# Grouped keys and queries of block 1's attention, loaded in pieces of 32 rows in place of 64

## The chip, the cores and the metric

The kernel runs on one core of one Trainium2 chip. Its time is the device time of one execution in microseconds (us); the times below are of three runs, with their median. The profile is of one further execution of the same kernel.

## What is computed

Three transformer blocks run one after the other on one sequence of 512 tokens with 1024 channels, all in float32. The change lies in the first. Its middle part projects the normalized input and runs two kinds of attention on it side by side, eight heads each:

```python
proj = h @ w_in[l]
qa, ka, va, qb, kb, vb = [proj[..., offs[i]:offs[i + 1]] for i in range(6)]
...
oa = diff_attention(qa[:, :, 0], qa[:, :, 1], ka[:, :, 0], ka[:, :, 1], va, lam, rel_bias)
...
qb = rms_norm(qb.reshape(B, S, N_HEADS_B, HEAD_DIM), q_norm[l]).transpose(0, 2, 1, 3)
kb = rms_norm(kb.reshape(B, S, N_KV_B, HEAD_DIM), k_norm[l]).transpose(0, 2, 1, 3)
qb = apply_rope(qb, cos, sin)
kb = apply_rope(kb, cos, sin)
ob = gqa_attention(qb, kb, vb).transpose(0, 2, 1, 3).reshape(B, S, D_MIX_B)
x = x + jnp.concatenate([oa, ob], axis=-1) @ w_out[l]
```

`gqa_attention` is the grouped one: eight query heads of 64 channels share two key heads, four to one. These grouped keys and queries are what the change loads in another way.

## The kernel before

Activations lie with channels on the 128 partitions and the 512 tokens along the row. Every float32 product is made of rounded parts: `weight` (L124) loads a weight panel into one of three `wraw` buffers, ScalarE rounds it to `whi` (L137), VectorE takes the rest as `wlo` (L138), and TensorE multiplies the parts in three matmuls (L120 to L122) that accumulate in a PSUM bank, named a to h.

Block 1's attention is `mix1` with `heads1` (from L563), some 240 us of the execution from about 420 us on. A head's operands go through DRAM, since matmul operands must lie on other partitions than the projection leaves them on. `parts` (L488) takes a projected and rotated chunk of 128 channels, writes its rounded value and its rest into a buffer `hl` (ScalarE L493, VectorE L494; there are two such buffers, `HL = 2`), and stores the buffer to DRAM (L499). The stored tensors are `qdd` and `kdd` for the first kind of attention, `qpd` and `kpd` for the grouped queries and keys; in each a row of DRAM is one channel, 512 values of the rounded part and then 512 of the rest. Operands are then loaded from there, one head ahead of their use:

- `keys` (L593) fills two `kg` tiles for a key head, one with the rounded parts, one with the rests, each with the head's 64 channels twice, on partitions 0 to 63 and 64 to 127.
- `ahead_gqa` (L678) fills a `qg` tile for a query head: rounded parts on partitions 0 to 63, rests on 64 to 127. On the first head of a group it calls `keys` before that.
- `operand` (L610) loads the `qd` and `kd` tiles of the first kind in pieces of 32 partitions (L614).

A head's 64 channels are 32 even ones and 32 odd ones, which lie 64 rows apart in DRAM. So one load of 64 partitions reads two runs of 32 rows; its access pattern `[(64, 2), (1, 32)]` says: 2 runs, 64 rows apart, of 32 rows, one apart. `part_rows` (L502) makes the pattern, with the 512 values of a row as the last dimension. Each load moves 64 rows of 2 KB, 128 KB. There are 8 loads of kg and 16 of qg.

The score matmuls are L627 (first kind, operands kd and qd) and L651 (grouped, operands kg and qg), both into banks a and b in turn. VectorE reduces the scores (L629, L652), ScalarE takes the exponential (L485). Beside the first heads run the value projections `v_tokens` (L505), into banks c to f, which ScalarE and VectorE empty into `vt` (L518, L519).

All of these loads and stores are issued by SyncE (SP), in one order. The order of the instructions on each engine is set by a scheduler when the kernel is built, and each engine then works through its own list. SP's DMAs take eight completion semaphores in turn, so that a DMA is issued only when the one eight places ahead of it has landed, beside what it waits for in its data and its buffer.

Of the kernel before, what the change touches and what calls it, by code (L numbers as in the profile page):

```python
# [29 lines left out]
def f32v(ap):  # L30
    return ap.bitcast(F32)


class K:
    NU = 5
    SECOND = ("dq", "pf", "ct", "cacc")
    out = "out"
# [525 lines left out]
    def heads1(self, xhl, rb, rtok, gq, ind, ocs):  # L563
        nc, D = self.nc, self.D
# [26 lines left out]
        d = []  # L591

        def keys(kv):  # L593
            ds = []
            for i in range(2):
                t = self.keep("kg", 3, F32R)
                for r in range(2):
                    nc.sync.dma_start(out=f32v(t[64 * r:64 * r + 64]), in_=self.part_rows(d[0], i, 32 * kv, [(64, 2), (1, 32)]))
                ds.append(t)
            return ds  # L600

# [55 lines left out]
        qds, kds, qgd = {}, {}, {}  # L657
# [20 lines left out]
        def ahead_gqa(c, r):  # L678
            if r == 0 and c % 2 == 0:
                kg[c // 2] = keys(c // 2)  # L680
            t = self.keep("qg", 2, F32R)
            for i in range(2):
                nc.sync.dma_start(out=f32v(t[64 * i:64 * i + 64]), in_=self.part_rows(qgd[c], i, 32 * r, [(64, 2), (1, 32)]))
            ops[4 + c, r] = t

        def mk_diff(c, r):
            if r == 1:
                qgd[c + self.AH] = rope(c + self.AH, "qpd") if c < 4 - self.AH else None
            ahead_gqa(c, r)
            return diff_head(2 * c + r, sms[c], *ops[c, r])  # L690
# [1434 lines left out]
```

## Time and profile before

| | us |
|---|---|
| median of three runs | 2681.27 |
| the three runs | 2675.64, 2681.27, 2682.28 |
| the profiled execution, its own time | 2672.23 |
| its span in the trace | 2670.5 |
| TensorE busy in it (PE) | 2596.1 |
| VectorE busy (DVE) | 1575.7 |
| ScalarE busy (ACT) | 1054.2 |
| GpSimd busy (POOL) | 403.6 |

Times in the trace are counted from the start of the span. PE stands for TensorE's matmuls, PEld for its weight loads, which overlap them; SPq is SyncE's queue, where the duration shown is that of issuing a DMA, not of its transfer. A row of the timeline has the start, the duration, the engine, the line of the kernel, the operation, its output and inputs, and, in square brackets, how long the engine was idle before it and whom it waited for. A row of the chain of waits has the start, the length and the piece of work that held up the end there. A row of a stretch has its length, the busy time and instruction count of each engine, then the granted TensorE clock as a share of full speed, the mean busy share of the core's 16 DMA engines, and the GB/s that they moved.

### The profile page before, as it was taken

How to read it: one execution, taken by the hardware profiler on the slowest of the kernel's cores; microseconds unless marked ns; L12 is line 12 of the kernel's file. 1: busy time of each engine (PE TensorE's matmuls, PEld its weight loads, DVE VectorE, ACT ScalarE, POOL GpSimd, SP SyncE). 2: the span in 40 equal slices, each digit the busy share in tenths (PEclk: the TensorE clock that was granted, in tenths of full speed). 3: DMA queues.
4: the chain of work that ended last, by engine and by line, in shares of the span. 5: the costliest groups of instructions: out<-in, count | busy, mean ns of one | idle time of the engine just before them, and what ended most of it. 6: DMA issues, size and time to landing. Idle time of an engine off the chain costs nothing.

```text
span 2670.5 us, 31163 instructions
## 1 busy us (share of the span) xinstructions
PE 2596.1 (97%) x11804; PEld 2097.3 (79%) x11804; DVE 1575.7 (59%) x2446; ACT 1054.2 (39%) x1621; POOL 403.6 (15%) x331
## 2 busy tenths in 40 slices
PE   8999998989999999999999999999899899999999
PEld 6887887767788887988788777888788777878787
DVE  7876655788644544467434854333545977746564
ACT  4222233676422324455323533223433464424242
POOL 1011012233000003133112201001210313101000
PEclk9999998989999999999999999999999999999999
DMA  5566644432632234431323342322524644323323
GB/s 196 178 200 202 205 155 148 138 104 96 209 95 95 88 102 134 137 111 65 97 99 128 134 144 93 97 96 96 187 69 149 209 103 158 95 91 94 99 88 111
DMA packets 114594, 340.00 MB, mean 127 GB/s; under 512 B 13784, under 2 KB 15768, under 8 KB 114314
## 3 DMA queue, kind: packets, MB, share of 16 engines
q1 hardware_dynamic: 104010, 301.02, 34.7%
q0 software_dynamic: 10432, 36.97, 4.4%
q8 instruction: 93, 1.52, 0.2%
q14 instruction: 59, 0.48, 0.1%
HBM read 301.47 MB, written 40.67 MB: 128 GB/s over the span
## 4 chain that ended last, share of the span: by engine, by line
PE 89%; DVE 5%; DMA 2%; ACT 2%; issue 1%; POOL 0%; SPq 0%; POOLq 0%; DVEq 0%; ACTq 0%
PE a L121 5%; PE a L120 5%; PE a L122 5%; PE e L122 4%; PE c L120 4%; PE c L122 4%; PE c L121 4%; PE e L120 4%; PE e L121 4%; PE f L120 4%; PE f L121 4%; PE f L122 4%; PE b L122 4%; PE b L120 4%; PE b L121 4%; PE d L120 4%
## 5 line engine op out<-in xcount | busy, mean ns | idle before, releaser
L137 ACT ACTIVATE whi<-wraw 128x1024 fp32r<-128x1024 f32 (+4 forms) x420 | 423.9, 1012 | 1048.5 <-PE e L121 172.2
L138 DVE TENSOR_TENSOR wlo<-wraw,whi 128x1024 fp32r<-128x1024 f32 (+5 forms) x408 | 494.7, 1214 | 326.0 <-ACT whi L137 320.1
L122 PE MATMUL e<-xh,wlo 128*128 128x512 f32 x368 | 144.1, 392 | 1.6 <-DVE wlo L138 1.6
L120 PE MATMUL e<-xh,whi 128*128 128x512 f32 x368 | 144.2, 392 | 0.0
L121 PE MATMUL e<-xl,whi 128*128 128x512 f32 x368 | 144.1, 392 | 0.0
L121 PE MATMUL a<-xl,whi 128*128 128x512 f32 x352 | 139.2, 396 | 2.3 <-DVE xl L194 2.0
L120 PE MATMUL a<-xh,whi 128*128 128x512 f32 x352 | 138.8, 394 | 0.2 <-ACT xh L911 0.2
L122 PE MATMUL a<-xh,wlo 128*128 128x512 f32 x352 | 138.1, 392 | 0.3 <-DVE wlo L138 0.3
L121 PE MATMUL c<-xl,whi 128*128 128x512 f32 x344 | 135.3, 393 | 2.5 <-DVE xl L194 2.5
L120 PE MATMUL c<-xh,whi 128*128 128x512 f32 x344 | 135.5, 394 | 0.9 <-ACT whi L137 0.9
L122 PE MATMUL c<-xh,wlo 128*128 128x512 f32 x344 | 135.0, 393 | 0.0
L120 PE MATMUL b<-xh,whi 128*128 128x512 f32 x304 | 119.7, 394 | 6.7 <-ACT xh L193 6.7
L121 PE MATMUL b<-xl,whi 128*128 128x512 f32 x304 | 119.7, 394 | 0.0
L122 PE MATMUL b<-xh,wlo 128*128 128x512 f32 x304 | 119.4, 393 | 0.0
L190 ACT ACTIVATE hh<-h 128x512 fp32r<-128x512 f32 x98 | 61.8, 630 | 144.0 <-DVE h L369 92.4
L122 PE MATMUL f<-xh,wlo 128*128 128x512 f32 x280 | 109.9, 392 | 0.6 <-DVE wlo L138 0.6
L942 POOL TENSOR_TENSOR acc<-sq 128x512 f32<-128x512 f32 x10 | 14.1, 1406 | 637.8 <-ACT sq L296 371.2
L120 PE MATMUL f<-xh,whi 128*128 128x512 f32 x280 | 110.2, 394 | 0.0
L121 PE MATMUL f<-xl,whi 128*128 128x512 f32 x280 | 109.3, 390 | 0.0
L122 PE MATMUL d<-xh,wlo 128*128 128x512 f32 x264 | 103.9, 394 | 2.0 <-DVE wlo L138 2.0
L120 PE MATMUL d<-xh,whi 128*128 128x512 f32 x264 | 104.3, 395 | 0.0
L121 PE MATMUL d<-xl,whi 128*128 128x512 f32 x264 | 103.7, 393 | 0.0
(1182 smaller groups left out, 6446.0 us busy)
## 6 DMA issues: line engine op xcount, KB each, us to landing
wraw<-w_up SPq DMA_DIRECT2D x76, 512.0 KB
mw<-w_mod POOLq DMA_DIRECT2D x48, 512.0 KB, 4.3
wraw<-ffn_w_gate SPq DMA_DIRECT2D x43, 512.0 KB
wraw<-ffn_w_up SPq DMA_DIRECT2D x43, 512.0 KB
wraw<-w_down SPq DMA_DIRECT2D x40, 512.0 KB
wraw<-ffn_w_down SPq DMA_DIRECT2D x32, 448.0 KB
wraw<-w_gate SPq DMA_DIRECT2D x24, 512.0 KB
wraw<-ffn_w_down SPq DMA_DIRECT2D x16, 512.0 KB
```

The costliest lines, as they stand in the source:

```text
L120: mm(out, ah, bh, start=(first and i == 0), stop=False)
L121: mm(out, ah, bl, start=False, stop=False)
L122: self.last_mm = mm(out, al, bh, start=False, stop=(last and i == n - 1)).ins
L137: nc.scalar.activation(hi[:, i:j], raw[:, i:j], AF.Copy)
L138: (nc.gpsimd if self.pool_lo else nc.vector).tensor_sub(lo[:, i:j], raw[:, i:j], f32v(hi[:, i:j]))
L190: nc.scalar.activation(hi, x, AF.Copy)
L942: i = (self.nc.vector if c == 6 else self.nc.gpsimd).tensor_add(a, acc, s).ins
```

## The change

Both loops issue two loads of 32 partitions for each that had 64, one for the even channels and one for the odd ones; what lands where is the same.

```diff
             for i in range(2):
                 t = self.keep("kg", 3, F32R)
                 for r in range(2):
-                    nc.sync.dma_start(out=f32v(t[64 * r:64 * r + 64]), in_=self.part_rows(d[0], i, 32 * kv, [(64, 2), (1, 32)]))
+                    for a in range(2):
+                        nc.sync.dma_start(out=f32v(t[64 * r + 32 * a:64 * r + 32 * a + 32]), in_=self.part_rows(d[0], i, 32 * kv + 64 * a, [(1, 32)]))
                 ds.append(t)
             return ds
...
             t = self.keep("qg", 2, F32R)
             for i in range(2):
-                nc.sync.dma_start(out=f32v(t[64 * i:64 * i + 64]), in_=self.part_rows(qgd[c], i, 32 * r, [(64, 2), (1, 32)]))
+                for a in range(2):
+                    nc.sync.dma_start(out=f32v(t[64 * i + 32 * a:64 * i + 32 * a + 32]), in_=self.part_rows(qgd[c], i, 32 * r + 64 * a, [(1, 32)]))
             ops[4 + c, r] = t
```

On TensorE, VectorE, ScalarE and GpSimd every instruction keeps its place (their lines below the edits count one or two higher). SP's list grows from 788 to 812 instructions. Its rows at the first grouped head, where kpd and qpd are stored and read back, were these before:

```order
L499 DMA kpd<-hl 128x1024
L598 DMA kg<-kpd 64x1x512 x4
L169 DMA wraw<-w_v 128x960
L598 DMA kg<-kpd 64x1x512 x2
L499 DMA qpd<-hl 128x1024
L499 DMA qdd<-hl 128x1024
L683 DMA qg<-qpd 64x1x512 x3
L169 DMA wraw<-w_v 128x640
L683 DMA qg<-qpd 64x1x512
L499 DMA kdd<-hl 128x1024
L169 DMA wraw<-w_in 128x1024
```

The same place in the changed kernel, with L598 now L599 and L683 now L685:

```order
L499 DMA kpd<-hl 128x1024
L599 DMA kg<-kpd 32x512 x8
L169 DMA wraw<-w_v 128x960
L599 DMA kg<-kpd 32x512 x4
L499 DMA qpd<-hl 128x1024
L499 DMA qdd<-hl 128x1024
L685 DMA qg<-qpd 32x512 x4
L169 DMA wraw<-w_v 128x640
L685 DMA qg<-qpd 32x512
L499 DMA kdd<-hl 128x1024
L685 DMA qg<-qpd 32x512 x3
L169 DMA wraw<-w_in 128x1024
```

Twelve pieces in place of six loads stand ahead of the store of qpd, and three of the second query head's four pieces have moved behind the store of kdd. Later, where the second key head is loaded, SP had these rows before:

```order
L620 DMA btab<-be_2029 128x896
L598 DMA kg<-kpd 64x1x512 x2
L683 DMA qg<-qpd 64x1x512 x2
L499 DMA qpd<-hl 128x1024
L614 DMA qd<-qdd 32x2x512 x3
```

And in the changed kernel:

```order
L621 DMA btab<-be_2029 128x896
L599 DMA kg<-kpd 32x512 x4
L685 DMA qg<-qpd 32x512 x4
L499 DMA qpd<-hl 128x1024
L615 DMA qd<-qdd 32x2x512 x3
```

Here eight pieces stand for four loads, and the order of the rest is as it was.

## The prediction

> **What bounds the kernel now.** I began with the page: its first line, the row of engines and the chain of what ended last.
>
> ```profile
> span 2670.5 us, 31163 instructions
> PE 2596.1 (97%) x11804; PEld 2097.3 (79%) x11804; DVE 1575.7 (59%) x2446; ACT 1054.2 (39%) x1621; POOL 403.6 (15%) x331
> ...
> PE 89%; DVE 5%; DMA 2%; ACT 2%; issue 1%; POOL 0%; SPq 0%; POOLq 0%; DVEq 0%; ACTq 0%
> ```
>
> TensorE sets the end; DMA holds 2% of the chain. A change that only touches loads can win no more than the places where TensorE stands still for one, directly or through another engine. So I read the chain in order of time over block 1's attention, about 420 to 660 us.
>
> ```profile
> 434.24 0.65 DVE hl L494 x2
> 434.88 13.18 DMA qpd<-hl
> 448.12 0.51 issue
> ```
>
> One DMA stands in the chain for 13.18 us: the store of the first rotated queries (qpd). It is no load that the diff touches, so the question is what made it slow. SP's queue in order of time:
>
> ```profile
> 421.82 0.33 SPq L499 DMA_DIRECT2D kpd<-hl  x1
> 426.42 2.56 SPq L598 DMA_DIRECT2D kg<-kpd  x4
> 429.09 1.97 SPq L169 DMA_DIRECT2D wraw<-w_v  x1
> 431.11 3.73 SPq L598 DMA_DIRECT2D kg<-kpd  x2
> 434.88 2.73 SPq L499 DMA_DIRECT2D qpd<-hl  x1
> 448.13 1.57 SPq L683 DMA_DIRECT2D qg<-qpd  x3
> ```
>
> The same kind of store, of kpd, was issued at 421.82, and the loads that read it left at 426.42: at most 4.6 us. The slow one was issued behind six kg loads. Now some stretches; the last three columns are TensorE's granted clock, the DMA share and GB/s:
>
> ```profile
> 426.40:427.90 1.50, 1.50 (x12) 1.50 (x12) 1.03 (x7) 0.30 (x1) 0.00 (x0) 1.00 0.07 3
> 435.00:438.00 3.00, 3.00 (x23) 2.96 (x21) 1.52 (x3) 2.09 (x3) 0.94 (x1) 1.00 0.13 49
> 441.00:445.00 4.00, 2.73 (x19) 2.46 (x17) 0.00 (x0) 0.00 (x0) 0.00 (x0) 1.00 0.13 49
> 455.00:460.00 5.00, 5.00 (x20) 4.90 (x19) 4.97 (x18) 2.16 (x6) 0.17 (x1) 0.50 0.71 233
> 460.00:461.00 1.00, 1.00 (x7) 0.91 (x6) 0.55 (x3) 0.45 (x2) 1.00 (x1) 0.86 0.34 67
> 526.00:531.00 5.00, 5.00 (x20) 3.71 (x19) 3.72 (x13) 2.87 (x8) 1.78 (x2) 0.75 0.86 244
> ```
>
> With kg loads in flight the share is 0.13, that is 2.1 of 16 DMA engines, at 49 GB/s. Six loads of 128 KB are 786 KB, and 786 KB at 49 GB/s take 16.0 us; counted from 427.90, where data begin to move, the two engines are free about 444, and two sixteenths of the store stand behind that. From 526 to 531 the queue holds loads of qd and kd, 32 partitions each, with a bias table: 0.86 and 244 GB/s.
>
> Who waits for the store? VectorE and ScalarE, then TensorE, whose next matmuls in its order need them:
>
> ```profile
> 437.35 0.74 ACT L137 ACTIVATE whi<-wraw 128x640 fp32r<-128x640 f32 x1 [0.42 <-PE f L122]
> 448.09 0.63 ACT L493 ACTIVATE hl<-af 128x512 fp32r<-128x512 f32 x1 [10.00 <-DMA qpd<-hl]
> ...
> 438.81 1.58 DVE L138 TENSOR_TENSOR wlo<-wraw,whi 128x640 fp32r<-128x640 f32 x1
> 448.75 0.69 DVE L494 TENSOR_TENSOR hl<-af,hl 128x512 fp32r<-128x512 f32 x1 [8.36 <-ACT hl L493]
> 450.16 0.16 DVE L635 RECIPROCAL rs<-sums 128x1 f32<-128x1 f32 x1 [0.48 <-ACT e L485]
> 453.84 0.54 DVE L519 SCALAR_TENSOR_TENSOR vt<-c,rr,vt 128x320 fp32r<-128x320 f32 x1
> 455.79 0.54 DVE L519 SCALAR_TENSOR_TENSOR vt<-d,rr,vt 128x320 fp32r<-128x320 f32 x1
> ...
> 443.42 0.31 PE L122 MATMUL f<-whi,xl 128*128 128x320 f32 x1
> 450.97 0.80 PE L627 MATMUL a<-kd,qd 96*128 96x512 f32 x1 [7.25 <-DVE mx L629]
> 454.43 0.64 PE L120 MATMUL c<-whi,xh 128*128 128x320 f32 x1 [2.06 <-DVE vt L519]
> 462.25 0.31 PE L120 MATMUL f<-whi,xh 128*128 128x320 f32 x1
> 462.40 0.31 PE L121 MATMUL f<-wlo,xh 128*128 128x320 f32 x1
> ```
>
> The hl buffers are two, so ScalarE's third split waits 10.00 us until the store has left one free; VectorE's subtraction of the same tile waits 8.36 us, with the score reduction behind it; TensorE stops 7.25 and 2.06 us. After the stop its clock is 0.50 (455 to 460), and 0.86 on average from 460 to 461, so full again from about 460.3.
>
> **The change, part by part.** The 24 loads of 64 partitions become 48 of 32. Bytes, tiles and the order on the four compute engines stay; only SP's queue grows.
>
> *The kg pieces ahead of the store.* Six loads become twelve. SP's time for them, by the nearest rows:
>
> ```profile
> 525.55 1.26 SPq L614 DMA_DIRECT2D qd<-qdd  x3
> 565.93 1.04 SPq L598 DMA_DIRECT2D kg<-kpd  x2
> 567.07 1.11 SPq L683 DMA_DIRECT2D qg<-qpd  x2
> 571.48 0.34 SPq L499 DMA_DIRECT2D qpd<-hl  x1
> ```
>
> 0.42 us each (1.26/3, 32 partitions, the same shape of piece) is my value; 0.64 (2.56/4, the kg loads in this very place) is the other end. Twelve take 5.0 to 7.7 us and the weight load between them about 0.5: from 426.42 SP is through at 431.9 to 434.6. The store's data are ready at 434.88 either way. If the pieces run like those of 526 to 531, their 786 KB take 786/244 = 3.2 us and nothing stands ahead of the store. It then takes at most the 4.6 us of kpd and lands by 439.5 instead of 448.06.
>
> *What is late next.* ScalarE is free at 438.09 (437.35 + 0.74) and can split at 439.5, done 440.1. VectorE is busy with wlo until 438.81 + 1.58 = 440.39, and this is the next limit: its subtraction starts at 440.39 instead of 448.75, all 8.36 us of the stop gone. The 0.48 us behind it was for ScalarE, which moves by 8.6 us (448.09 to 439.5), so I take about half of it, 0.25. TensorE's score matmul could start at 450.97 − 8.6 = 442.4, before TensorE is through at 443.73: that stop is gone. The c matmuls, which wait for vt, start at 454.43 − 8.6 = 445.8; a stop of some 1.6 us stays there.
>
> *The clock.* If the clock stays full, the work from 454.43 to 460.3, 5.85 us at half speed, needs half, a gain of 2.9. VectorE's vt for bank d comes 1.95 us after c's (455.79 − 453.84) whatever the clock. Ten c matmuls at 0.15 (462.40 − 462.25) and one score matmul, by its 512 columns against 320 an estimated 0.24, take 1.7. So 0.2 to 0.4 comes back, and 2.6 stays.
>
> The sum is 8.36 + 0.25 + 2.6 = 11.2 us at the point where bank f starts (462.25). Its upper end is TensorE without a wait: from 443.73, five score matmuls of 0.24 and thirty of 0.15 take 5.7, so 462.25 becomes 449.4, a gain of 12.8. Its lower end, with the clock down as before, is 8.6.
>
> *The other loads.* They hold up stores and weights in the same way, but nobody on the path waits for those:
>
> ```profile
> 460.00:480.00 20.00, 20.00 (x123) 18.66 (x122) 9.72 (x16) 8.72 (x17) 3.38 (x4) 0.99 0.55 192
> ...
> SPq L614 <- PE b L627: 40.9, 5, 10.5
> ```
>
> TensorE is busy for all of 460 to 480, and the view of waits lists none of its waits from 480 to 660 as one for a DMA, so landing earlier is worth 0. On the cost side stand 24 more issues by 0.42 to 0.56 us, 10 to 13 us of SP's time. SP itself waits 40.9 us for TensorE before the qd loads, so that it is hidden. The tightest place is 565.93: eight pieces instead of four end at 565.93 + 8 × 0.54 = 570.3, before the store that waits for its data until 571.48. Without that cover it would be 1 to 2 us.
>
> A rule of the Trainium skill speaks against this change: "DMA: Bandwidth & Descriptors", section "Rules for kernel authors", says of two transfers to disjoint halves of the partitions "Don't bother — they serialize", and that under 64 KB one pays mostly overhead. By it the sum above would be 0 or a loss; the rows above (2.1 engines for the 64-partition loads) speak against its premise that both halves use all sixteen. The same page's "How many engines (k)", in the section on the semaphore's 16, takes the largest count up to 16 that divides the slowest dimension of both sides, by which the source's leading 2 gives two engines and the new 32 gives sixteen.
>
> **The rivals.**
>
> *The clock drops all the same (0.24).* For the 1.6 us stop that stays there are rows on both sides:
>
> ```profile
> 508.64 0.50 PE L473 MATMUL f<-ptl,vt 128*128 128x512 f32 x1 [1.42 <-DVE ptl L471]
> 500.00:510.00 10.00, 8.58 (x47) 6.88 (x46) 9.32 (x25) 6.09 (x16) 6.73 (x6) 1.00 0.44 125
> ...
> 581.88 0.73 PE L651 MATMUL b<-kg,qg 128*128 128x512 f32 x2 [0.66 <-ACT e L485]
> 580.00:590.00 10.00, 8.86 (x33) 6.69 (x32) 7.55 (x18) 6.89 (x17) 2.32 (x2) 0.66 0.40 114
> ```
>
> A stop of 1.42 us left the clock at 1.00; another of 0.66 lies in a stretch with 0.66, which is 6.8 us at half speed (10 × 0.34 / 0.5). One such stretch costs up to 3.4 us, two, as VectorE-bound heads come later, up to 6.8. The gain is then 11.2 − 3.4 = 7.8 or 4.4: 2673.5 or 2676.9. "TensorE: Matmul & The Clock Gate", Part 1, of the Trainium skill lets the clock fall only after an idle window of about 3.4 us; the row of 0.66 us does not agree with it.
>
> *SP becomes late (0.06).* At 1.0 us for each piece (the row of 429.09 shows 1.97 for one issue) SP is through at 438.9 and the store lands at 443.8; the DVE gate moves from 440.39 to 444.4, and the gain is about 7: 2674.
>
> *The pieces stay on two engines (0.04), and the kernel is slower.* Then the change doesn't do what it says. The data still need the 16.0 us, and every added piece pays a start: 1.5 us from the issue to the first data (0.07 and 3 GB/s from 426.40 to 427.90). Six added starts ahead of the store, unhidden, are 9 us: 2690. It decides as soon as the pieces move at 49 GB/s. The 244 GB/s of other 32-partition loads speak against it. If the starts overlap, the time stays as it is (0.04 more): 2681.
>
> **How the numbers follow.** The profiled execution took 2672.23 us, 1.7 more than its span; the median of the runs is 2681.27, 9.0 above it. I take the same microseconds off: 2672.23 − 11.2 = 2661.0 for a profiled execution, 2681.27 − 11.2 = 2670.1 for the median. About 0.3% (8.0 us) is what a measurement of this kernel can tell from no change; the runs shown lie 6.6 us apart. The forecast has 0.62, the clock 0.24, SP 0.06, no spreading 0.08. Of the forecast's chance 0.06 goes to "same", since its low end lies at 8.6; of the clock's, 0.08 goes to "faster", where one short stretch costs little. That gives faster 0.62 − 0.06 + 0.08 = 0.64, same 0.06 + 0.16 + 0.06 + 0.04 = 0.32 and slower 0.04. The range runs from a gain of 20 (the 12.8, and the 6.6 by which runs differ) to one of 3 (the two stretches of clock, and a little of that spread): 2661 to 2678.
>
> **What would show it.** Right: no qpd store in the chain; the share with kg pieces in flight far above 0.13; the waits of 10.00, 8.36 and 7.25 us gone; the f matmul of 462.25 about 11 us earlier; the clock at 1.00 from 440 to 460. Wrong: a share of 0.13 beside kg; a store that still takes over 8 us; new PE waits for kg or qg; or more half-speed stretches between 500 and 600 than before.

## The result, and the profile after

| | before | changed |
|---|---|---|
| median, us (five runs each) | 2679.84 | 2661.26 |
| lowest and highest | 2674.26 to 2682.28 | 2659.24 to 2664.79 |
| the profiled execution, its own time | 2672.23 | 2659.24 |
| its span | 2670.5 | 2657.4 |
| granted clock over it, mean | 0.987 | 0.991 |

The ratio is 0.9938, with an interval of 0.9921 to 0.9955: faster by 16.6 us, between 12 and 21. The 16.6 is the distance of the means (2678.66 and 2662.06); the medians in the table lie 18.6 apart.

The page of the changed kernel, its first line, the row of engines and the summary of the chain:

```profile
span 2657.4 us, 31196 instructions
PE 2589.6 (97%) x11804; PEld 2091.7 (79%) x11804; DVE 1576.3 (59%) x2446; ACT 1053.3 (40%) x1621; POOL 402.0 (15%) x331
...
PE 88%; DVE 5%; ACT 2%; DMA 2%; issue 1%; POOL 0%; SPq 0%; DVEq 0%; ACTq 0%; POOLq 0%
```

The shares hardly move, as 13 us of 2670 cannot show in whole per cents. SP's queue in order of time does show the change:

```profile
421.99 0.33 SPq L499 DMA_DIRECT2D kpd<-hl  x1
426.54 3.60 SPq L599 DMA_DIRECT2D kg<-kpd  x8
...
430.65 1.82 SPq L599 DMA_DIRECT2D kg<-kpd  x4
435.04 0.34 SPq L499 DMA_DIRECT2D qpd<-hl  x1
...
438.19 1.71 SPq L685 DMA_DIRECT2D qg<-qpd  x4
```

The twelve pieces are issued by 432.47 (430.65 + 1.82), at 0.45 us each (3.60/8). The store of qpd goes out at 435.04, and the loads that read it at 438.19, so it took at most 3.15 us where it had taken 13.18. In the chain in order of time no DMA stands between 420 and 470 us.

What was in flight, as stretches of the changed kernel; the last three columns are the granted clock, the DMA share and GB/s:

```profile
430.00:434.00 4.00, 2.20 (x17) 1.95 (x16) 2.07 (x4) 1.26 (x2) 0.00 (x0) 1.00 0.76 223
435.00:438.00 3.00, 3.00 (x13) 3.00 (x12) 1.27 (x3) 1.58 (x3) 0.77 (x1) 0.50 0.72 288
440.00:460.00 20.00, 19.38 (x128) 18.38 (x128) 15.29 (x38) 11.55 (x25) 7.08 (x6) 1.00 0.63 204
```

And one stretch of the kernel before, for the last of these:

```profile
440.00:460.00 20.00, 10.70 (x47) 9.42 (x46) 11.12 (x32) 9.07 (x21) 3.00 (x3) 0.67 0.38 130
```

With kg pieces in flight the share is 0.76 in place of 0.13. From 440 to 460 us TensorE now works 19.38 us of 20 at full clock, in place of 10.70 at 0.67. The clock of 0.50 from 435 to 438 is new, and is taken up below. The engines of the changed kernel, in order of time:

```profile
439.05 0.74 ACT L137 ACTIVATE whi<-wraw 128x640 fp32r<-128x640 f32 x1 [1.95 <-PE f L122]
439.69 0.61 ACT L493 ACTIVATE hl<-af 128x512 fp32r<-128x512 f32 x1
...
440.51 0.82 DVE L138 TENSOR_TENSOR wlo<-wraw,whi 128x640 fp32r<-128x640 f32 x1
441.25 0.69 DVE L494 TENSOR_TENSOR hl<-af,hl 128x512 fp32r<-128x512 f32 x1
...
433.27 0.41 PE L120 MATMUL e<-whi,xh 128*128 128x320 f32 x1 [1.80 <-DVE af L608]
446.51 0.41 PE L120 MATMUL c<-whi,xh 128*128 128x320 f32 x1 [0.62 <-DVE vt L519]
452.01 0.31 PE L120 MATMUL f<-whi,xh 128*128 128x320 f32 x1
```

The waits of 10.00 us (ScalarE's split), 8.36 us (VectorE's subtraction) and 7.25 us (TensorE's score matmul) have no successor: the split follows whi at once, the subtraction follows wlo at once. The f matmul that began at 462.25 begins at 452.01.

To compare kernels without what happened ahead of the place, I count from the issue of the store of kpd to this first f matmul, and call the difference the **gain in the stage**. Before it is 462.25 − 421.82 = 40.43 us, in the changed kernel 452.01 − 421.99 = 30.02: a gain of 10.4. The two profiled executions differ by 2672.23 − 2659.24 = 13.0; the other 2.6 lie outside the stage.

### The profile page after: what moved, and what is told of

It reads as the page before. It is cut to its first block, busy times and chain, and to the rows that moved or that the text cites. A ratio compares the mean times of both kernels' runs of the same rounds, so it can differ in the third digit from the quotient of the medians.

```text
span 2657.4 us, 31196 instructions
## 1 busy us (share of the span) xinstructions
PE 2589.6 (97%) x11804; PEld 2091.7 (79%) x11804; DVE 1576.3 (59%) x2446; ACT 1053.3 (40%) x1621; POOL 402.0 (15%) x331
## 4 chain that ended last, share of the span: by engine, by line
PE 88%; DVE 5%; ACT 2%; DMA 2%; issue 1%; POOL 0%; SPq 0%; DVEq 0%; ACTq 0%; POOLq 0%
PE e L122 5%; PE a L120 5%; PE a L122 5%; PE a L121 5%; PE e L120 4%; PE e L121 4%; PE c L120 4%; PE c L122 4%; PE c L121 4%; PE f L120 4%; PE f L121 4%; PE f L122 4%; PE b L122 4%; PE b L120 4%; PE b L121 4%; PE d L120 4%
```

## The experiments

The experiments set four theories against each other. A: the price is the kg loads' small number of DMA engines, which holds up the store that is queued behind them. B: the qg loads, or the later heads, bring part of the gain. C: the size or the number of the DMAs decides, not how many engines they use. D, from the second group on: the whole price is the hl buffer that the late store keeps. The first four kernels share 26 runs of the kernel before (median 2676.17 us, 2666.88 to 2686.68), the other four share 24 (2676.64, 2664.83 to 2683.29). A count of runs stands with each median.

**Only the kg loads in pieces.**

```diff
-                    nc.sync.dma_start(out=f32v(t[64 * r:64 * r + 64]), in_=self.part_rows(d[0], i, 32 * kv, [(64, 2), (1, 32)]))
+                    for a in range(2):
+                        nc.sync.dma_start(out=f32v(t[64 * r + 32 * a:64 * r + 32 * a + 32]), in_=self.part_rows(d[0], i, 32 * kv + 64 * a, [(1, 32)]))
```

> Only the kg loads are in pieces of 32 rows; the qg loads are as before. Theory A (the six kg loads ahead of the qpd store held it up, nothing else counts): the store takes under 5 us in the chain in place of 13.18, the f matmul that stood at 462.25 comes 10 to 12 us earlier, and the time falls by as much as with the whole change, 12 to 17 us. Rival B (the qg loads and the later heads give a good part of the 16.6 us): the time falls by 6 to 11 us only.

Measured: 2663.09 us (8 runs), ratio 0.9954 (0.9934 to 0.9975). SP's queue:

```profile
438.35 0.34 SPq L499 DMA_DIRECT2D qpd<-hl  x1
...
441.48 1.67 SPq L684 DMA_DIRECT2D qg<-qpd  x3
```

The store takes at most 3.1 us, though all qg loads are as before. From the store of kpd (425.31) to the first f matmul (454.38) are 29.07 us: a gain in the stage of 11.4. The kg edit alone brings the gain of the whole change.

**Only the qg loads in pieces.**

```diff
-                nc.sync.dma_start(out=f32v(t[64 * i:64 * i + 64]), in_=self.part_rows(qgd[c], i, 32 * r, [(64, 2), (1, 32)]))
+                for a in range(2):
+                    nc.sync.dma_start(out=f32v(t[64 * i + 32 * a:64 * i + 32 * a + 32]), in_=self.part_rows(qgd[c], i, 32 * r + 64 * a, [(1, 32)]))
```

> Only the qg loads are in pieces of 32 rows; the kg loads are as before. Theory A: the store still takes about 13 us in the chain, and the time stays within 3 us of before. Rival B: the time falls by 4 to 8 us, with fewer half-speed stretches of TensorE's clock between 480 and 600 us.

Measured: 2677.9 us (12 runs), ratio 1.0011 (0.9995 to 1.0027). Its chain in order of time, then VectorE's wait:

```profile
436.60 13.02 DMA qpd<-hl
```

```profile
450.30 0.69 DVE L494 TENSOR_TENSOR hl<-af,hl 128x512 fp32r<-128x512 f32 x1 [8.21 <-ACT hl L493]
```

The store and the wait behind it are as long as before, and the gain in the stage is 0.5 (463.42 − 423.50 = 39.92). B falls: sixteen qg loads of the old kind cost nothing that shows on the path, and the low end of the interval leaves their pieces a gain of 1.3 us at most.

**64 partitions as before, but sixteen engines.** The pattern's two dimensions change places, so that its slowest one counts 32 in place of 2, in both loops. The rows then land in another order (even and odd channels alternate, in keys and queries alike); size, number and place of the DMAs are those of the kernel before.

```diff
-                    nc.sync.dma_start(out=f32v(t[64 * r:64 * r + 64]), in_=self.part_rows(d[0], i, 32 * kv, [(64, 2), (1, 32)]))
+                    nc.sync.dma_start(out=f32v(t[64 * r:64 * r + 64]), in_=self.part_rows(d[0], i, 32 * kv, [(1, 32), (64, 2)]))
...
-                nc.sync.dma_start(out=f32v(t[64 * i:64 * i + 64]), in_=self.part_rows(qgd[c], i, 32 * r, [(64, 2), (1, 32)]))
+                nc.sync.dma_start(out=f32v(t[64 * i:64 * i + 64]), in_=self.part_rows(qgd[c], i, 32 * r, [(1, 32), (64, 2)]))
```

> Loads of 64 partitions as before, as many and in the same order on every engine, but the source pattern walks its 32 rows in the outer dimension and the 2 runs in the inner one (the channels of a head lie in another order on the partitions, for keys and queries alike). Theory A (the number of DMA engines that a load runs on decides): a DMA share far above 0.13 while kg loads are in flight, a store under 5 us, and the time of the whole change, 12 to 17 us below before. Rival C (the size or the number of the loads decides): a share of 0.13 and no gain, within 3 us of before.

Measured: 2662.53 us (7 runs), ratio 0.9949 (0.9929 to 0.9969). SP's queue, and a stretch with kg loads in flight:

```profile
425.48 2.52 SPq L598 DMA_DIRECT2D kg<-kpd  x4
...
428.68 1.15 SPq L598 DMA_DIRECT2D kg<-kpd  x2
433.73 0.33 SPq L499 DMA_DIRECT2D qpd<-hl  x1
...
436.45 1.81 SPq L683 DMA_DIRECT2D qg<-qpd  x3
```

```profile
428.00:431.00 3.00, 2.16 (x16) 1.91 (x14) 0.38 (x1) 0.00 (x0) 0.00 (x0) 1.00 0.82 250
```

Loads of the same 128 KB, as many as before, run at a share of 0.82 and 250 GB/s; the store takes at most 2.7 us, and the gain in the stage is 11.4 (449.76 − 420.69 = 29.07). C falls: neither size nor number decides. What the change really alters is the slowest dimension of the pattern.

**Four narrow kg loads in place of six.** The changed kernel, but the first of the two kg tiles of a key head is loaded in the old way. Of the six narrow loads ahead of the store four stay, and the other two become four pieces.

```diff
                 for r in range(2):
+                    if i == 0:
+                        nc.sync.dma_start(out=f32v(t[64 * r:64 * r + 64]), in_=self.part_rows(d[0], i, 32 * kv, [(64, 2), (1, 32)]))
+                        continue
                     for a in range(2):
```

> The change, but the first kg tile of each key head is loaded in the old way: four old loads of the six ahead of the qpd store. Theory A, in proportion: 4 x 131 KB at 49 GB/s are 10.7 us from 427.9, so the two engines are free at 438.6, the store takes 6 to 8 us in the chain, and VectorE's subtraction comes 1 to 3 us later than with the whole change, so the time falls by 9 to 15 us. Rival C: the two old loads that stand last hold the store as long as six did, 12 to 13 us, and the gain is under 4 us.

Measured: 2672.48 us (12 runs), ratio 0.9993 (0.9978 to 1.0008). Its chain:

```profile
431.92 0.60 SPq L599
432.57 8.28 DMA kg<-kpd
440.92 8.24 DMA qpd<-hl
```

The store takes 8.24 us, between 13.18 and 3.15, as A has it. VectorE still stands 4.02 us for it, and the gain in the stage is 4.2 (463.43 − 427.24 = 36.19), about 7 less than the full change has. The sizes were missed: from the store of kpd, VectorE's subtraction starts 22.6 us on (449.85 − 427.24), 4.1 later than in the change (443.67 − 425.15 = 18.5 in its second execution, shown below) in place of the 1 to 3 expected, and the time, which should have fallen by 9 to 15 us, is not told from that of before. By the time alone C's "under 4 us" would fit as well; the store's 8.24 us, where C has 12 to 13, speaks against C. One reason for the missed sizes stands in the chain: the store is issued only when the second narrow load, eight places ahead of it, has landed (432.57 + 8.28 = 440.85), about 0.6 us after its data (VectorE's part of the buffer is done at 440.26).

**Four narrow kg loads, by one kg buffer fewer.** The loads are the old ones, but with two kg tiles the load of the third must wait for a tile, and so stands behind the store.

```diff
-                t = self.keep("kg", 3, F32R)
+                t = self.keep("kg", 2, F32R)
```

> The old loads of 64 partitions, but two kg tiles in place of three, so that four old kg loads instead of six stand ahead of the qpd store, and all four of the second key head come later. Theory A (the store waits for what the two DMA engines still have to move): 4 x 131 KB at 49 GB/s are 10.7 us from 427.9, with the store's own share free at about 440, so the store takes 7 to 8 us in the chain in place of 13.18 and VectorE's subtraction comes 5 to 6 us earlier than before; the f matmul of 462.25 comes 6 to 9 us earlier. Near 576 the four late kg loads cost 2 to 3 us of it. The time falls by 3 to 8 us. Rival C (the size of the loads, not what is ahead of the store): the store takes 12 to 13 us as before, and the time does not fall.

Measured: 2670.8 us (10 runs), ratio 0.9977 (0.9963 to 0.9990). Its chain, SP's queue and the list of waits:

```profile
439.20 8.01 DMA qpd<-hl
```

```profile
431.00 2.62 SPq L598 DMA_DIRECT2D kg<-kpd  x4
...
439.20 0.33 SPq L499 DMA_DIRECT2D qpd<-hl  x1
```

```profile
ACT hl L493 <- DMA qpd<-hl: 3.3, 1, 3.3
...
DVE hl L494 <- ACT hl L493: 2.4, 1, 2.4
```

And TensorE, where it first needs the loads that have been put off:

```profile
578.18 0.72 PE L651 MATMUL a<-kg,qg 128*128 128x512 f32 x1 [2.64 <-DMA kg<-kpd]
```

No instruction is added here and no DMA is cut; two narrow loads have gone from ahead of the store to behind it, and it takes 8.01 us. The queue's arithmetic fits: four loads of 128 KB at the 49 GB/s of the kernel before are 10.7 us, from 432.5 (431.00 and the 1.5 us to the first data) to 443.2, and the store lands 4 us after that, at 447.2; with six loads it was 444 and 448.1. The gain in the stage is 5.5 (461.12 − 426.16 = 34.96), a little under the 6 to 9 expected; the clock stood at 0.50 from 438.4 to 441.6 us in this execution, as it does in the first one of the changed kernel. The loads put off cost 2.64 us near 578, within the 2 to 3 expected.

**Three hl buffers, with the old loads.** If the store only hurts by keeping an hl buffer, a third buffer should win what the change wins. The room for it is taken from another buffer (xa), which is used elsewhere.

```diff
-    HL = 2
+    HL = 3
...
-            x = self.keep("xa", 3)
+            x = self.keep("xa", 1)
```

> The old loads, with three hl buffers in place of two (and one xa buffer in place of three, to make room), so that the third split needn't wait for the qpd store. Theory A2 (the late store reaches TensorE on two ways, the hl buffer and the qg loads that read it back): the waits of 10.00 and 8.36 us are gone, the store still takes 12 to 13 us, and the first grouped score matmul now waits for the qg loads until about 457, so the f matmul of 462.25 comes only 2 to 5 us earlier. Rival D (the buffer was the whole price): no wait for qg, 10 to 12 us earlier. The time: 0 to 4 us below before by A2, 9 to 13 by D; the single xa buffer may cost a few us after 600.

Measured: 2676.01 us (10 runs), ratio 0.9995 (0.9978 to 1.0011). Its chain, and TensorE in order of time:

```profile
435.66 12.88 DMA qpd<-hl
448.55 0.50 SPq L683
449.11 8.12 DMA qg<-qpd
```

```profile
445.28 0.41 PE L120 MATMUL c<-whi,xh 128*128 128x320 f32 x1 [0.61 <-DVE vt L519]
...
457.31 1.19 PE L651 MATMUL b<-kg,qg 128*128 128x512 f32 x2 [8.29 <-DMA qg<-qpd]
```

ScalarE and VectorE no longer wait for the store. Counted from the store of kpd (issued at 422.64 here), TensorE starts its c matmuls after 22.64 us, where the kernel before took 454.43 − 421.82 = 32.61: it is 10.0 us ahead. Then it stands 8.29 us for the first grouped queries, which are read back from the same late store by loads that need 8.12 us themselves. The first f matmul starts at 460.97, a gain in the stage of 2.1 (460.97 − 422.64 = 38.33), at the low end of the 2 to 5 expected; TensorE still runs at half clock there (0.50 from 457 to 462), and by the fourth f matmul (463.13, and 463.57 before) the lead is 41.75 − 40.49 = 1.3 us. D, which has 10 to 12 us here, falls. What the single xa buffer costs later is not separated from this in the time. The late store reaches TensorE on two ways, by the buffer and by the read back, and shortening the store is what shortens both.

**The changed kernel and the sixteen-engine form again,** on another chip. The first is the changed kernel, the second repeats the third experiment.

> The changed kernel itself once more. If the 11.4 us by which the two other kernels without old kg loads ahead of the store came earlier in this place are all there is, the time lies 9 to 14 us below before in this comparison; if the first result's 16.6 us hold, 15 us or more. The half-speed time of TensorE's clock is expected within 15 us of that of the other kernels without the long store.

> The loads of 64 partitions on sixteen engines once more, beside the changed kernel on the same chip. If SP's 24 added issues are hidden, both have the same time within 3 us; if they cost what they take, 10 to 13 us of SP's time, this kernel is faster by more than 3 us.

Measured: the changed kernel 2668.28 us (7 runs), ratio 0.9966 (0.9948 to 0.9984); the other form 2665.26 us (6 runs), 0.9951 (0.9935 to 0.9967). The changed kernel's rows in this execution, and a stretch:

```profile
425.15 0.33 SPq L499 DMA_DIRECT2D kpd<-hl  x1
...
442.14 1.60 DVE L138 TENSOR_TENSOR wlo<-wraw,whi 128x640 fp32r<-128x640 f32 x1
443.67 0.68 DVE L494 TENSOR_TENSOR hl<-af,hl 128x512 fp32r<-128x512 f32 x1
448.13 0.54 DVE L519 SCALAR_TENSOR_TENSOR vt<-c,rr,vt 128x320 fp32r<-128x320 f32 x1
...
436.43 0.41 PE L120 MATMUL e<-whi,xh 128*128 128x320 f32 x1 [1.80 <-DVE af L608]
448.72 0.42 PE L120 MATMUL c<-whi,xh 128*128 128x320 f32 x1 [1.18 <-DVE vt L519]
454.22 0.31 PE L120 MATMUL f<-whi,xh 128*128 128x320 f32 x1
```

```profile
430.00:450.00 20.00, 17.02 (x115) 16.15 (x113) 14.44 (x36) 11.32 (x23) 6.64 (x6) 1.00 0.64 211
```

From the store of kpd to the first f matmul are 454.22 − 425.15 = 29.07 us, to the hundredth what the kg edit alone and the third experiment have, and the sixteen-engine form again has 452.79 − 423.72 = 29.07. So 11.4 us is the gain in the stage of all three forms wherever the clock stays full there. It is still there near the end of the attention: the matmul of L473 that starts at 661.23 us before starts at 652.97 in this execution, 239.41 and 227.82 us behind the store of kpd, a gain of 11.6 (10.0 to 14.0 over the five executions of the three forms). The whole span is only 2.7 us shorter than that of the profiled execution before (2667.8 and 2670.5), since this execution came to the place 3.3 us later, and lost 5.6 us of its lead behind the attention, where the change touches nothing. So a single pair of executions does not size the change by its spans. The ratio of 0.9966 is 9.1 us, in the 9 to 14 expected, and its interval leaves out the 15 of the other reading. The mean clock, 0.988, is that of the other two kernels (0.987 and 0.988 in the first and third experiment), so its half-speed time is no other. Whether the 24 added issues cost anything elsewhere is not settled: the mean of all 12 runs of the changed kernel is 2664.9 us, of all 13 of the sixteen-engine form 2662.2, and 2.7 us apart is less than twice the standard error of that difference (about 1.5). That form is no slower, with half the DMAs.

## Why the prediction was right

**The cause.** Right. The 13.18 us of the store came from six kg loads on few engines (0.13 of sixteen, about two) ahead of it. Removing the narrowness in pieces (first experiment) or in place (third) brings the store to about 3 us, and four narrow loads leave 8.0 to 8.2. The prediction took 4.6 for the store, the bound from kpd's; 1.5 us too long, without effect, since VectorE's wlo ends later.

**The sum.** The second profiled execution of the changed kernel has no half-speed stretch in the stage, and is set 3.33 us late (425.15 against 421.82). With that taken off, VectorE's subtraction starts at 440.34, where 440.39 was predicted: the 8.36 term. From there to vt are 4.46 us (443.67 to 448.13), where they were 5.09 (448.75 to 453.84): 0.63 in place of the 0.25 taken; 0.48 of it is the reciprocal's wait, which is gone as a whole. The clock's term is what is left of 11.36, some 2.3 for the 2.6 predicted. Terms of 8.4, 0.6 and 2.3 stand against 8.36, 0.25 and 2.6: 11.4 measured, 11.2 predicted. That the sum agrees better than its second and third terms is luck, since one was too small by about as much as the other was too large.

**The stop that stays.** It was put at 1.6 us before the c matmuls; it is 1.18 here and 0.62 in the first execution. The list of TensorE's waits no longer has the score matmul's 7.25.

**The other loads and the issues.** Worth 0, as predicted: the second experiment's 1.0011. The tightest place on SP came out as worked out. In the changed kernel's queue at the second key head:

```profile
554.04 1.70 SPq L599 DMA_DIRECT2D kg<-kpd  x4
556.16 1.83 SPq L685 DMA_DIRECT2D qg<-qpd  x4
559.38 0.34 SPq L499 DMA_DIRECT2D qpd<-hl  x1
```

The pieces are through at 557.99, and the store waits for its data until 559.38: 1.4 us of cover, predicted 1.2. The list of waits has none of TensorE's from 480 to 660 us for a DMA.

**The rivals.** SP did not become late, and the pieces did not stay on two engines (0.76 against 0.13). The clock did not drop behind the 1.6 us stop, where the first rival had it. It dropped once in another place, from 434.8 us in the first profiled execution, behind a stop of 1.80 us ahead of bank e's matmuls. Against the second execution that is 11.36 − 10.41 = 0.95 us in the stage, where the rival had up to 3.4 for one such stretch: the f matmuls ran at half speed, ScalarE's whi came 1.5 us late (439.05 less the shift of 0.17, against 437.35), and VectorE made up part of it (its wlo took 0.82 in place of 1.58, see below). The part from 500 to 600, named as a place where the clock could show the forecast wrong, in the kernel before and then in the changed one:

```profile
500.00:600.00 100.00, 89.03 (x407) 63.55 (x406) 83.08 (x217) 69.18 (x163) 34.41 (x27) 0.86 0.33 103
```

```profile
500.00:600.00 100.00, 89.79 (x440) 64.19 (x439) 85.98 (x222) 73.70 (x173) 31.78 (x24) 0.91 0.33 102
```

The clock is 0.91 where it was 0.86, and in the second execution of the changed kernel it is 0.86 again, so nothing was given back there.

**The two rules.** "DMA: Bandwidth & Descriptors" of the Trainium skill, section "Rules for kernel authors", advises against two transfers to disjoint halves of the partitions, because both use all sixteen engines. For these loads the reason is not given (the old ones ran at 0.13 of sixteen), and the runs do not agree with the rule: the kg split alone gives 0.9954 (0.9934 to 0.9975). The same page's "How many engines (k)" takes the count from the slowest dimension of both sides, which here gives two engines for the old pattern and sixteen for the piece of 32. The runs agree, and more sharply than the change could show: with the dimensions swapped and nothing else, the share goes from 0.13 to 0.82.

**The size of the result.** 16.6 us were measured at first where 11.2 were predicted, and the median of 2661.26 lies 8.8 us below the 2670.1 forecast. The five runs of the kernel before lay high and the five of the changed kernel low. Over all runs of this study the kernel before has a mean of 2676.1 us (55 runs) and the changed kernel one of 2664.9 (12 runs): 11.2 us apart, with an interval of about 2.5 to either side. So the gain was not off, as far as these runs can tell. Of the 8.8 us, 5.2 are the base: the median of three runs, 2681.27, from which 11.2 was taken off, was that far above the mean of the 55. The other 3.6 are the low draw of the five changed runs. That the median still fell inside the range of 2661 to 2678, by 0.26 us, was luck.

## What to carry to other kernels

A short stall for a store is worth tracing back along the DMA queue: look at the share of DMA engines while the transfers ahead of it are in flight, and if it is near one or two sixteenths (here 0.13), look at the slowest dimension of their access patterns. Put the large count first there (here 32 before 2): that needs no further DMAs, and was no slower here than splitting. The rows then land in another order, so both operands of a product must be loaded in the same one. Split where the order cannot be changed. Before giving a late store another buffer, ask who reads the stored data back, since that reader waits for the same store.

## What the runs showed of the hardware

**Narrow loads hold up wide stores.** A store that spreads over the engines takes about 3 us with wide loads ahead of it (2.7 to 3.15), 8.0 to 8.2 with four narrow ones, and 12.9 to 13.2 with six, although the mean DMA share is only 0.13 meanwhile in the kernel before.

**VectorE's subtraction took twice as long beside GpSimd.** The same 128x640 wlo took 1.60 us in the second execution of the changed kernel (442.14, above), and 0.82 in the first (440.51). GpSimd's rows near it, of the second and then of the first:

```profile
441.78 1.28 POOL L585 TENSOR_TENSOR rot<-ra,rot 128x512 f32<-128x512 f32 x1
```

```profile
438.60 1.29 POOL L585 TENSOR_TENSOR rot<-ra,rot 128x512 f32<-128x512 f32 x1
442.24 1.57 POOL L639 TENSOR_SCALAR e<-e,rs 128x512 f32<-128x512 f32 x1 [2.35 <-DVE rs L636]
```

In the second, GpSimd works until 443.06, for the first 0.92 us of the subtraction; in the first it is idle from 439.89 to 442.24, all through it. The ten traces hold twenty subtractions of this shape in this stage: the seven with GpSimd idle take 0.82 to 0.83 us, and the thirteen that begin while it works for another 0.90 to 1.13 us take 1.58 to 1.81. No run took GpSimd's work away, so that the one causes the other is likely and not shown.

**The clock does not fall the same way each time.** The stop of 1.80 us ahead of bank e's matmuls stands in the rows of both executions of the changed kernel above; it was followed by a clock of 0.50 in the first (435 to 438) and of 1.00 in the second (430 to 450). The kernel before had the same stop, and full clock behind it; its rows, the matmul and then a stretch:

```profile
433.09 0.41 PE L120 MATMUL e<-whi,xh 128*128 128x320 f32 x1 [1.80 <-DVE af L607]
```

```profile
434.00:438.00 4.00, 4.00 (x30) 3.96 (x28) 2.52 (x5) 2.73 (x4) 0.94 (x1) 1.00 0.15 52
```

Nine of the ten profiled executions have this stop of 1.80 us, and the clock fell within 2 us behind it in two of them, the first one of the changed kernel and the one with two kg tiles. "TensorE: Matmul & The Clock Gate", Part 1, of the Trainium skill lets the clock fall only after an idle window of about 3.4 us; the stop of 1.80 us in the first execution does not agree with it. What decides stays open.

**Runs spread with the clock.** The 50 later runs of the kernel before lie between 2664.83 us at a mean granted clock of 0.989 and 2686.68 at 0.982; 0.007 of 2670 us is 18.7 of the 21.9 us between them. The gain of this change, 0.4%, is half of that spread, and five runs of each did not size it. A distance in the trace sized it in its stage: it repeats to 0.01 us where the clock stays full (29.07 in four executions), and was 30.02 in the one where it did not.
